# The last retention head's norm behind the combinations of the normalized input, and weight preparation behind copies of partial sums

## The chip, the cores and the metric

The kernel runs on one core of one Trainium2 chip. The metric is the device time of one execution in microseconds (us). TensorE is called PE in the profile, VectorE DVE, ScalarE ACT, GpSimd POOL and SyncE, which issues the transfers, SP.

## The reference, cut to what matters

One inference step of one decoder layer, for a prompt of 512 tokens and 8 single new tokens with states of their own. The kernel treats them as one matrix of N = 520 columns with 1024 channels.

```python
h = rms_norm(r, norm_mix_g)
rq, rk, rv, rg, gq, gf, gi, gg, a_ret, a_hg = split(h @ w_in)
o_r, s_ret = retention_chunked(rotary(rq), rotary(rk), rv, ...)       # 4 heads of 128 x 256
u_r = (o_r * rsqrt(mean(o_r * o_r) + EPS) * ret_norm_g * silu(rg)) @ w_up_ret
o_g, s_hg = gla_chunked(silu(gq), 1 - f, gi, log f, ...)              # 8 heads of 128 x 128
u_g = (o_g * rsqrt(mean(o_g * o_g) + EPS) * hg_norm_g * silu(gg)) @ w_up_hg
m = sigmoid(a_ret) * u_r + sigmoid(a_hg) * u_g
r = r + m @ w_o
r = r + square(relu(rms_norm(r, norm_mlp_g) @ w_ff1)) @ w_ff2
r = r + sigmoid(rms_norm(r, norm_ple_g) @ w_ple_gate) * (p_l @ w_ple_proj)
y = rms_norm(r, norm_final_g)
```

All of it is in float32. The change concerns the norm of the fourth retention head (in u_r), and the products for the two gates a_ret and a_hg.

## The kernel before

**Layout.** Activations lie with channels on the 128 partitions and the 520 columns along the free axis. A matrix product is made of units: one unit takes a 1024 x 128 block of a weight matrix, in 8 slots of 128 rows each. Weights and activations are each cut into a rounded half (H, wh) and the rest (L, wl); a product is wh*H + wh*L + wl*H, and the 520 columns go in two halves, so a slot is 6 matmuls and a unit 48 (`mm`, L232).

**Preparation.** A unit's weights arrive by a transfer into one of three `raw` buffers, and are then cut by `prep`: ScalarE copies them rounded into `wh` (L210) and VectorE subtracts (L215, `wl`). There are three `wh` and three `wl` buffers, and preparation runs two entries ahead of the product. After the cut the next transfer is issued.

**Pairs.** Some products (the gates a_ret and a_hg, and three quarters of ff1) are done two 128-column blocks at once with fewer multiplications (a Strassen-Winograd scheme). `sums` (L855 to L858) makes four combinations of the activations; `h_sums(kp)` does so for the normalized input, in five calls kp = 0 to 4: one adds H and L back together into `hn` (L942), forms the combinations into `hs`, and a call later cuts them into the two halves `hc` (rounded on ScalarE at L938, the rest on VectorE at L944). The tiles of `hc` lie in the places S8 and S9, S11 and S15, S13 and S14, S10 and S12. A pair runs in four steps, `run_pair(n, 0)` to `run_pair(n, 3)`, of 24, 24, 24 and 12 matmuls (`product`, L866); partial results X, Y and Z lie in PSUM. In step 0 ScalarE copies X (L881) and Z (L883) out, in step 1 it copies X again (L886) and VectorE adds Y to the first copy (L889), in step 2 VectorE subtracts X (L892), then the older copy of X from Z (L896). The next product that accumulates into X must wait until X has been read. The weights of each step are combinations too: `prep_pair` adds on VectorE (L172, into scratch space in `cst`), cuts on ScalarE (L166) and subtracts on VectorE (L168). `P.part` and `P.done` finish a result: for a gate a tanh (L967), and for a_hg a product on VectorE (L972); for ff1 relu (L1132), square (L1136) and a split (L587, L588).

**Order.** The order of the work is written out by hand: each engine runs its instructions in the order of the program text. `flow` lists units and steps of pairs. `at[u]` lists functions that run in the middle of unit u, after four of its slots, in the order in which they were appended. `run_unit` first prepares weights, then runs half the product, then the functions of `at[u]`, then the other half, and last the copy of the result out of PSUM. A set `prep_last` names steps of pairs that prepare weights in their middle and not at their start; before the change it holds step 2 of all eight gate pairs, and step 2 of the one ff1 pair that is followed by no ff2 unit in that step.

**Around the change.** Retention's heads 0 to 3 run in two groups P of two heads e. A head's last steps are `rt_out` (squares into `sq`, the gated result into `t`, both temporaries in the places S12 and S10), `rt_ext` (the 8 decode columns, then the split of the squares), `rt_norm` (a sum over partitions by four matmuls with ones, L579 and L580, then Ln, L569, and Exp, L571) and `rt_scale` (`t` times the result, L808, and its split, L587 and L588, into `orH` and `orL`). For head 3 these fall into the units of the first up-projection, `u_hg` to `u_hg + 4`, in whose middles the `h_sums` stand as well: `rt_norm` and `rt_scale` of head 3 and `h_sums(3)` stand in this order in `u_hg + 4`, `h_sums(4)` in `u_hg + 5`. Directly after that unit comes step 0 of the first gate pair. The up-projection's units copy their result into `xT` (L915), whose old content has been saved to DRAM (`xpark`). ScalarE holds one table of functions at a time; where an instruction needs another, a table load is put ahead of it, and `S.preload_act_table_set` puts one where it is called.

Of the kernel before, what the change touches and what calls it, by code (L numbers as in the profile page):

```python
# [19 lines left out]
N = T + NB  # L20
# [25 lines left out]
def decoder_step_kernel(  # L46
# [27 lines left out]
    V, S, G, PE = nc.vector, nc.scalar, nc.gpsimd, nc.tensor  # L74
# [13 lines left out]
    cst = cp.tile([128, C_END], F32, name="cst")  # L88
# [16 lines left out]
    def full(tag, dt=F32, name=None):  # L105
        return big.tile([128, 8, N], dt, tag=tag, name=name or tag)

    def pair(tag, name, dt=F32):
        return big.tile([128, 2, N], dt, tag=tag, name=name)

    def bank():
        return pss.tile([128, 512], F32, tag="s", name="s")
# [5 lines left out]
    at = defaultdict(list)  # L118
    extra = set()
    prep_last = set()  # L120
# [67 lines left out]
    def prep(engines=None, apart=False):  # L188


        if done["prep"] >= len(seq):
            return
        engines = engines or [(S, V)]
        u = seq[done["prep"]]
        done["prep"] += 1
        if not isinstance(u, int):
            prep_pair(*u)
            return
        r = raw_of.pop(u)
        if u in w_tags:  # L200
            wh, wl = (big.tile([128, 8, 128], F32R, tag=t, name="w6") for t in w_tags[u])
        else:
            wh = wp.tile([128, 8, 128], F32R, tag="wh", name="wh")
            wl = wp.tile([128, 8, 128], F32R, tag="wl", name="wl")
        w_of[u] = (wh, wl)
        n = 8 // len(engines)
        for i, (e0, e1) in enumerate(engines):
            k = slice(n * i, n * (i + 1))
            if e0 is S:
                S.activation(wh[:, k], r[:, k], AF.Copy)  # L210
            else:
                e0.tensor_copy(wh[:, k], r[:, k])
            if apart:
                yield
            e1.tensor_sub(wl[:, k], r[:, k], wh[:, k])  # L215
            if i < len(engines) - 1:
                yield
        load()

    def prep_all():  # L220
        for _ in prep():
            pass
# [52 lines left out]
    xT = full("B0", name="xT")  # L275
# [310 lines left out]
    def split(H, L, x):  # L586
        S.activation(H, x, AF.Copy)  # L587
        V.tensor_sub(L, x, H)  # L588
# [47 lines left out]
    rt = {}  # L636
# [120 lines left out]
    def rt_out(P, e):  # L757
        def go():
            hd = 2 * P + e
            vn, Sst, Q, g = rt["vn"], rt["S"], rt["Q", P][:, e], rt["g"]  # L760
            A = rt["A"][:, 0, 0:512]
            dma(ret_prompt[0, 0, hd], Sst[:, 3, :])
            sq = pair("S12", "rsq")
            t = pair("S10", "rt")
            for z in range(2):
                j = 2 * hd + z
                b = bank()
                zs = slice(z * 128, (z + 1) * 128)
                for c in range(4):
                    cs = slice(c * 128, (c + 1) * 128)  # L770
                    PE.matmul(b[:, cs], lhsT=vn[:, c, zs], rhs=A[:, cs], start=True, stop=c == 0)  # L771
                    if c:
                        PE.matmul(b[:, cs], lhsT=Sst[:, c - 1, zs], rhs=Q[:, cs], start=False, stop=True)
                S.activation(sq[:, z, 0:T], b, AF.Square)
                V.scalar_tensor_tensor(t[:, z, 0:T], in0=b, scalar=retg[:, j:j + 1], in1=g[:, z, 0:T],
                                       op0=ALU.mult, op1=ALU.mult)
                V.tensor_scalar(t[:, z, T:N], g[:, z, T:N], retg[:, j:j + 1], None, op0=ALU.mult)
            rt["sq"], rt["t"] = sq, t
        return go
# [14 lines left out]
    def rt_norm(P, e):  # L794
        def go():
            hd = 2 * P + e
            sq, t = rt["sq"], rt["t"]
            bs = ones_bc(rt["sqH"][:, 0], rt["sqH"][:, 1])
            r = sq[:, 0]
            rsqrt(r, bs, 1.0 / 256)  # L800
            rt["ng"] = t, r
        return go

    def rt_scale(P, e):
        def go():
            hd = 2 * P + e
            t, r = rt["ng"]
            V.tensor_tensor(t, t, r.unsqueeze(1).to_broadcast([128, 2, N]), op=ALU.mult)  # L808
            orH[hd] = pair(OSLOT[hd], "orH", F32R)
            orL[hd] = pair(f"S{4 + hd}", "orL", F32R) if hd else og["b"][:, 4:6]  # L810
            split(orH[hd], orL[hd], t)
        return go

    for P in range(2):
        b = len(units)
        for e in range(2):
            unit(W, RK + (2 * P + e) * 128, hk, hl, ev_rope(P, e, "K", KSCALE))
        for e in range(2):
            unit(W, RQ + (2 * P + e) * 128, hk, hl, ev_rope(P, e, "Q", 1.0))
        for e in range(2):  # L820
            for base, ev in ((RV, ev_rv), (RG, ev_rg)):
                for z in range(2):
                    unit(W, base + (2 * P + e) * 256 + z * 128, hk, hl, ev(P, e, z))
        for e in range(2):
            o = b + 4 * e
            at[o + 5].append(rt_scores(P, e))
            at[o + 6].append(rt_kT(P, e))
            at[o + 6].append(rt_vT(P, e))
            at[o + 7].append(rt_state(P, e))
            at[o + 8].append(rt_dec_add(P, e, 0))  # L830
            at[o + 9].append(rt_dec_add(P, e, 1))
            at[o + 10].append(rt_dec_out(P, e))
            at[o + 11].append(rt_ext(P, e))
            at[o + 12].append(rt_norm(P, e))
            at[o + 12].append(rt_scale(P, e))
        for e in range(2):
            at[b + 4 * e + 8].append(rt_out(P, e))

# [30 lines left out]
    def run_pair(n, i):  # L869

        P = pairs[n]
        if (n, i) not in prep_last:
            prep_all()
        if i == 0:
            P.t = P.begin()
            P.X, P.Z = bank()[:, 0:NH], bank()[:, 0:NH]
        X, Z = P.X, P.Z
        t1, t2 = P.t[:, 0], P.t[:, 1]
        if i == 0:
            product(n, 0, 0, "A11", X, True)  # L880
            S.activation(r1, X, AF.Copy)  # L881
            product(n, 0, 1, "S1", Z, True)
            S.activation(t2[:, z1], Z, AF.Copy)  # L883
        elif i == 1:
            product(n, 1, 0, "S2", X, False)
            S.activation(t2[:, z0], X, AF.Copy)  # L886
            Y = bank()[:, 0:NH]
            product(n, 1, 1, "A12", Y, True)
            V.tensor_tensor(t1[:, z0], r1, Y, op=ALU.add)  # L889
        elif i == 2:  # L890
            product(n, 2, 0, "S3", X, False)
            V.tensor_tensor(t2[:, z1], t2[:, z1], X, op=ALU.subtract)  # L892
            if (n, i) in prep_last:
                prep_all()
            product(n, 2, 1, "S4", Z, False)
            V.tensor_tensor(t2[:, z0], Z, t2[:, z0], op=ALU.subtract)  # L896
            P.part(1, slice(0, N), t2)
            P.done(1)
        else:
            P.part(0, z0, t1[:, z0])  # L900
            product(n, 3, 0, "A22", X, False)
            P.part(0, z1, X)
            P.done(0)
# [29 lines left out]
    def h_sums(kp):  # L933

        def go():
            if kp > 0:
                H, L = hc[kp - 1] = tuple(big.tile([128, 4, NH], F32R, tag=t, name="hc") for t in HTAGS[kp - 1])
                S.activation(H, hc["t"], AF.Copy)  # L938
            if kp < 4:
                n = pair("X2", "hn")  # L940
                for h in range(2):
                    V.tensor_tensor(n[:, h], hH[:, kp + 4 * h], hL[:, kp + 4 * h], op=ALU.add)  # L942
            if kp > 0:
                V.tensor_sub(L, hc["t"], H)  # L944
            if kp < 4:
                hc["t"] = big.tile([128, 4, NH], F32, tag="X0", name="hs")
                sums(hc["t"], n)
        return go
# [31 lines left out]
    u_hg = len(units)  # L980
# [4 lines left out]
        unit(w_up_ret[0], j * 128, lambda k: orH[k // 2][:, k % 2], lambda k: orL[k // 2][:, k % 2], ev_ur(j))  # L985
    for kp in range(5):
        at[u_hg + 1 + kp].append(h_sums(kp))
    flow += range(u_hg, u_hg + 6)
    gates = [gate_pair(j, c, c == A_RET) for j in range(4) for c in (A_RET, A_HG)]
    for n, u in zip(gates, [u_hg + 6, u_hg + 7, *range(u_ret, u_ret + 6)]):  # L990
        flow += [(n, 0), u, (n, 1), (n, 2), (n, 3)]
        prep_last.add((n, 2))
    flow += [u_ret + 6, u_ret + 7]


# [396 lines left out]
    for c in range(4):  # L1392
        t = big.tile([128, D], F32, tag=f"S{12 + c}", name=f"xn{c}")
# [79 lines left out]
    hd = pair("S1", "hd")[:, 0, 0:64].rearrange("p (k t) -> p k t", k=8)  # L1473
# [165 lines left out]
```

## Time and profile before

| | |
|---|---|
| median of 3 runs | 1101.16 us (1100.19 to 1101.61) |
| profiled execution, its own time | 1101.45 us |
| span of its profile, first to last instruction | 1099.6 us |
| mean granted clock of TensorE | 0.996 of full speed |
| busy: PE, DVE, ACT | 1081.8, 712.9, 509.7 us |
| the stage of the change: last up-projection units and gate pairs | about 440 to 612 us |

The profile is one execution. Its engines run side by side, so that busy times do not add up to the span: the engine that is busy nearly all the time sets it, and an idle time of another engine matters only where that engine ends up waiting for it. A row of a timeline gives the start of an instruction from the span's start, its length, the engine, the line of the kernel, the operation, the tile written and the tiles read; in brackets stands how long the engine had been idle before, and what ended that.

### The profile page before, as it was taken

The page shows a single profiled execution, that of the slowest core. Times are in us where ns is not written, and L with a number is a line of the kernel's source. Part 1 is how long each engine was busy: PE and PEld are TensorE (multiplying, and loading weights), DVE is VectorE, ACT ScalarE, POOL GpSimd, SP SyncE. Part 2 cuts the span into 40 slices and gives each one's busy share as a digit, 9 for nine tenths or more (in the row PEclk, how much of TensorE's full clock was granted, in tenths as well). Part 3 has the DMA queues.
Part 4 walks back from the last instruction along what each step waited for, and adds up shares of the span by engine and source line. Part 5 has one row for each costly group of instructions (what it writes and reads, how often), then busy time and mean ns, then how long its engine had stood idle before and what let it go on. Part 6 is the DMA issues. An engine that isn't in the chain of part 4 may idle for free.

```text
span 1099.6 us, 23412 instructions
## 1 busy us (share of the span) xinstructions
PE 1081.8 (98%) x10193; PEld 1061.1 (96%) x10193; DVE 712.9 (65%) x1113; ACT 509.7 (46%) x853; POOL 23.9 (2%) x19
## 2 busy tenths in 40 slices
PE   8999999999999999989999999999999999999997
PEld 8999999999999999989999999999999999999997
DVE  6566776858664854866677656776656665654565
ACT  6323534334254333555444335445555445544555
POOL 1000000000011011000000000000000000000001
PEclk9999999999999999999999999999999999999999
DMA  7556252443356456412343432232332332344302
GB/s 222 154 175 174 83 162 75 136 121 109 113 157 171 120 154 179 120 58 90 104 134 109 142 93 81 77 97 77 116 96 83 112 113 78 96 135 116 97 20 79
DMA packets 211847, 127.30 MB, mean 116 GB/s; under 512 B 4104, under 2 KB 209168, under 8 KB 211488
## 3 DMA queue, kind: packets, MB, share of 16 engines
q1 hardware_dynamic: 211744, 125.80, 38.8%
q8 instruction: 80, 1.31, 0.5%
q14 instruction: 23, 0.19, 0.1%
HBM read 112.02 MB, written 13.76 MB: 114 GB/s over the span
## 4 chain that ended last, share of the span: by engine, by line
PE 91%; DVE 5%; ACT 2%; issue 1%; DMA 0%; DVEq 0%; SPq 0%; ACTq 0%
PE m L232 57%; PE s L866 17%; PE m L1364 2%; PE s L1364 2%; PE s L369 1%; DVE wl L215 1%; PE s L488 1%; DVE comb L1070 1%; ACT wh L210 1%; PE s L549 1%; PE s L525 1%; PE s L771 1%; PE s L728 1%; PE s L232 1%; PE s L551 0%
## 5 line engine op out<-in xcount | busy, mean ns | idle before, releaser
L215 DVE TENSOR_TENSOR wl<-raw,wh 128x1024 fp32r<-128x1024 f32 (+1 forms) x125 | 155.4, 1245 | 80.2 <-ACT wh L210 79.4
L232 PE MATMUL m<-hH,wh 128*128 128x260 f32 x864 | 179.1, 289 | 0.0
L232 PE MATMUL m<-hH,wl 128*128 128x260 f32 x864 | 174.4, 283 | 0.0
L232 PE MATMUL m<-hL,wh 128*128 128x260 f32 x864 | 173.8, 283 | 0.0
L210 ACT ACTIVATE wh<-raw 128x1024 fp32r<-128x1024 f32 (+1 forms) x125 | 130.5, 1046 | 56.0 <-PE m L232 52.0
L232 PEld LDWEIGHTS m<-hH,wh 128*128 128x128 f32 x864 | 132.9, 189 | 2.5 <-issue 0.8
L232 PEld LDWEIGHTS m<-hH,wl 128*128 128x128 f32 x864 | 133.1, 188 | 0.0
L232 PEld LDWEIGHTS m<-hL,wh 128*128 128x128 f32 x864 | 133.1, 188 | 0.0
L866 PE MATMUL s<-comb,wh 128*128 128x260 f32 x672 | 122.4, 283 | 0.5 <-DVE comb L1070 0.5
L866 PEld LDWEIGHTS s<-comb,wh 128*128 128x128 f32 x672 | 103.9, 188 | 0.7 <-DVE comb L1070 0.7
L866 PE MATMUL s<-comb,wl 128*128 128x260 f32 x336 | 95.1, 283 | 0.0
L166 ACT ACTIVATE wh<-cst 128x512 fp32r<-128x512 f32 x80 | 50.5, 631 | 74.1 <-DVE cst L172 60.8
L232 PE MATMUL m<-fa,wh 128*128 128x260 f32 x384 | 67.0, 283 | 0.5 <-ACT fa L587 0.5
L232 PE MATMUL m<-oga,wh 128*128 128x260 f32 x384 | 65.5, 286 | 0.0
L168 DVE TENSOR_TENSOR wl<-cst,wh 128x512 fp32r<-128x512 f32 x80 | 55.2, 690 | 13.3 <-ACT wh L166 10.3
L866 PEld LDWEIGHTS s<-comb,wl 128*128 128x128 f32 x336 | 63.2, 188 | 0.0
L232 PEld LDWEIGHTS m<-oga,wh 128*128 128x128 f32 x384 | 54.7, 192 | 0.8 <-issue 0.8
L232 PEld LDWEIGHTS m<-fa,wh 128*128 128x128 f32 x384 | 54.7, 188 | 0.7 <-ACT fa L587 0.7
L866 PE MATMUL s<-hc,wh 128*128 128x260 f32 x256 | 48.8, 287 | 4.8 <-ACT hc L938 2.3
L232 PE MATMUL m<-fh,wl 128*128 128x260 f32 x256 | 51.3, 282 | 0.5 <-DVE wl L215 0.5
L232 PE MATMUL m<-fh,wh 128*128 128x260 f32 x256 | 51.6, 283 | 0.0
L232 PE MATMUL m<-fa,wl 128*128 128x260 f32 x256 | 51.5, 283 | 0.0
(375 smaller groups left out, 2322.8 us busy)
## 6 DMA issues: line engine op xcount, KB each, us to landing
raw<-in_w_in_dram SPq DMA_DIRECT2D x56, 512.0 KB, 4.3
raw<-in_w_ff_dram SPq DMA_DIRECT2D x40, 512.0 KB, 4.0
rawp<-in_w_ff_dram SPq DMA_DIRECT2D x24, 512.0 KB, 3.6
vbc<-vdd SPq DMA_DIRECT2D x16, 512.0 KB, 4.2
rawp<-in_w_in_dram SPq DMA_DIRECT2D x16, 512.0 KB, 4.6
Sd<-in_state_hgrn_dram SPq DMA_DIRECT2D x8, 512.0 KB, 5.5
out_dram<-Sd SPq DMA_DIRECT2D x8, 512.0 KB, 5.2
rSd<-in_state_ret_dram SPq DMA_DIRECT2D x8, 512.0 KB, 6.6
```

The lines of the kernel that those rows point to most:

```text
L166: S.activation(wh[:, 4 * h:4 * h + 4], x, AF.Copy)
L168: V.tensor_sub(wl[:, 4 * h:4 * h + 4], x, wh[:, 4 * h:4 * h + 4])
L210: S.activation(wh[:, k], r[:, k], AF.Copy)
L215: e1.tensor_sub(wl[:, k], r[:, k], wh[:, k])
L232: PE.matmul(ps[z], lhsT=a[:, k, :], rhs=b[:, z * NH:(z + 1) * NH], start=first and i == 0, stop=last and i == 2)
L369: PE.matmul(b[32 * j:32 * j + 32, 32 * hc:32 * hc + 32], lhsT=kx[:, h, o:o + 32], rhs=qx[:, h, o:o + 32], start=True, stop=True)
L488: PE.matmul(b[32 * i:32 * i + 32, :], lhsT=q[g], rhs=Sd[g][:, 4 * z:4 * z + 4, :], start=True, stop=True)
L525: PE.matmul(b[:, c * 128:(c + 1) * 128], lhsT=kn[:, h, c, :], rhs=vn[:, h, c, :], start=True, stop=True)
L549: PE.matmul(o, lhsT=vn[:, h, c, :], rhs=A[:, h * 4 + c, :], start=True, stop=c == 0)
L728: PE.matmul(b[:, c * 256:(c + 1) * 256], lhsT=kn[:, 2 * i + c, :], rhs=vn[:, 2 * i + c, :], start=True, stop=True)
L866: PE.matmul(out, lhsT=w[:, 4 * half + k, :], rhs=x, start=start and k == 0 and m == 0, stop=k == 3 and m == 2, skip_group_check=not start)
L1364: PE.matmul(ps, lhsT=w[:, k, :], rhs=x, start=k == 0 and n == 0, stop=k == 7 and n == 2)
```

## The change

It does four things. For head 3 the temporaries `sq` and `t` go from S12 and S10 into a stretch of `cst` whose constants have been used up and into rows 6 and 7 of `xT`. `rt_norm` and `rt_scale` of head 3 are appended after the `h_sums`: the norm behind `h_sums(3)` in `u_hg + 4`, the scaling behind `h_sums(4)` in `u_hg + 5`. Two table loads are written out, one in `u_hg + 1` with Ln and Exp, one after the scaling with the set that the gates' tanh uses. And in gate pairs step 1 also prepares weights in its middle, behind the copy L886; for every step 2 in `prep_last`, which includes the one ff1 pair, `P.part(1, ...)` and `P.done(1)` move from the end of step 2 into step 3, behind the preparation there.

```diff
@@ rt_out
-            sq = pair("S12", "rsq")
-            t = pair("S10", "rt")
+            if hd == 3:
+                sq = cst[:, 512:512 + 2 * N].rearrange("p (a n) -> p a n", a=2)
+                t = xT[:, 6:8]
+            else:
+                sq, t = pair("S12", "rsq"), pair("S10", "rt")
@@ the retention units
-            at[o + 12].append(rt_norm(P, e))
-            at[o + 12].append(rt_scale(P, e))
+            if P == 0 or e == 0:
+                at[o + 12].append(rt_norm(P, e))
+                at[o + 12].append(rt_scale(P, e))
@@ run_pair
             product(n, 1, 0, "S2", X, False)
             S.activation(t2[:, z0], X, AF.Copy)
+            if (n, i) in prep_last:
+                prep_all()
             Y = bank()[:, 0:NH]
...
             V.tensor_tensor(t2[:, z0], Z, t2[:, z0], op=ALU.subtract)
-            P.part(1, slice(0, N), t2)
-            P.done(1)
+            if (n, i) not in prep_last:
+                P.part(1, slice(0, N), t2)
+                P.done(1)
         else:
+            if (n, 2) in prep_last:
+                P.part(1, slice(0, N), t2)
+                P.done(1)
             P.part(0, z0, t1[:, z0])
@@ the up-projection and the gates
     for kp in range(5):
         at[u_hg + 1 + kp].append(h_sums(kp))
+    at[u_hg + 1].append(lambda: S.preload_act_table_set("natural_log_exp_and_others"))
+    at[u_hg + 4].append(rt_norm(1, 1))
+    at[u_hg + 5].append(rt_scale(1, 1))
+    at[u_hg + 5].append(lambda: S.preload_act_table_set("exp_and_others"))
...
-        prep_last.add((n, 2))
+        prep_last |= {(n, 1), (n, 2)}
```

## The prediction

> **What bounds the kernel now.** I read the page first, then the waits of TensorE, then the timelines of the places that these waits name. The first column of a timeline is the start in us from the span's start, the second the time from the first start to the last end of the row; the bracket is the idle time before it and what ended it.
>
> ```profile
> span 1099.6 us, 23412 instructions
> PE 1081.8 (98%) x10193; PEld 1061.1 (96%) x10193; DVE 712.9 (65%) x1113; ACT 509.7 (46%) x853; POOL 23.9 (2%) x19
> ```
>
> TensorE (PE) is busy for 1081.8 of 1099.6 us. The change takes no matmul away, so it can win only from TensorE's waits, or from time in which its matmuls run slowly. Its waits, over the whole span and then (last line) its weight loads from 476 to 620 us:
>
> ```profile
> PE s L866 <- ACT hc L938: 2.3, 1, 2.3
> PE s L866 <- DVE hc L944: 1.9, 2, 1.0
> ...
> PE m L232 <- DVE wl L215: 0.5, 1, 0.5
> ```
>
> ```profile
> PEld s L866 <- ACT gt L886: 1.9, 6, 0.3
> ```
>
> Three places appear: one long stop on the combinations `hc` (L938 is the rounded half, L944 the rest), six equal stops on the copy in L886, and one on a weight preparation (L215). The change touches the queues ahead of all three. The waits understate what each costs, so I size each by its period on TensorE. These are starts of matmuls of the gate pairs:
>
> ```profile
> 476.79 0.28 PE L866 MATMUL s<-hH,wh 128*128 128x260 f32 x1
> ...
> 482.98 0.39 PE L866 MATMUL s<-hc,wh 128*128 128x260 f32 x1 [2.26 <-ACT hc L938]
> ...
> 491.84 0.40 PE L866 MATMUL s<-hc,wh 128*128 128x260 f32 x2
> ...
> 499.03 0.28 PE L866 MATMUL s<-hH,wh 128*128 128x260 f32 x1
> ...
> 507.69 0.40 PE L866 MATMUL s<-hc,wh 128*128 128x260 f32 x2
> ```
>
> From 476.79 to 491.84 TensorE runs step 0 of the first pair and one unit, 24 + 48 = 72 matmuls, in 15.05 us. From 499.03 to 507.69 it runs the same 72 of the second pair in 8.66 us, 0.120 each. **The first stop costs 15.05 - 8.66 = 6.39 us.**
>
> Why it stops is on VectorE (DVE) and ScalarE (ACT), here in order of time on each:
>
> ```profile
> 470.05 0.69 DVE L168 TENSOR_TENSOR wl<-cst,wh 128x512 fp32r<-128x512 f32 x1
> 474.16 1.24 DVE L808 TENSOR_TENSOR rt<-rt,rsq 128x1040 f32<-128x1040 f32 x1 [3.42 <-ACT rsq L571]
> 476.54 1.24 DVE L588 TENSOR_TENSOR orL<-rt,orH 128x1040 fp32r<-128x1040 f32 x1 [1.14 <-ACT orH L587]
> 477.70 1.31 DVE L942 TENSOR_TENSOR hn<-hH,hL 128x520 f32<-128x520 f32 x2
> ...
> 481.34 0.43 DVE L858 TENSOR_TENSOR hs<-hs,hn 128x260 f32<-128x260 f32 x1
> 481.68 1.22 DVE L215 TENSOR_TENSOR wl<-raw,wh 128x1024 fp32r<-128x1024 f32 x1
> 482.96 1.24 DVE L944 TENSOR_TENSOR hc<-hs,hc 128x1040 fp32r<-128x1040 f32 x1
> ```
>
> ```profile
> 470.04 1.28 ACT L569 ACT_TABLE_LOAD   x1
> ...
> 472.19 1.28 ACT L571 ACT_TABLE_LOAD   x1
> 473.49 0.64 ACT L571 ACTIVATE rsq<-rsq 128x520 f32<-128x520 f32 x1
> ...
> 476.41 1.06 ACT L938 ACTIVATE hc<-hs 128x1040 fp32r<-128x1040 f32 x1
> 477.38 0.58 ACT L915 ACTIVATE xT<-m 128x520 f32<-128x520 f32 x1
> ...
> 481.86 1.07 ACT L938 ACTIVATE hc<-hs 128x1040 fp32r<-128x1040 f32 x1 [2.95 <-DVE hs L858]
> ```
>
> Retention's last norm (Ln, Exp, the product in L808, the split in L588) sits ahead of the fourth `hn` sum. VectorE idles 3.42 us for the Exp, behind two table loads, and 1.14 us for ScalarE's half of the split. The last combination is done at 482.96 + 1.24 = 484.20, while TensorE wants it soon after 479.
>
> **Part 1, the norm behind the combinations.** Nothing ahead of 470.05 moves. The temporaries of head 3 now lie in `cst` and `xT`, so the last `hc` tiles in S10 and S12 do not wait for the norm; all earlier readers of those places are over. From there I lay the same instructions out again with the same durations. VectorE: the block L942 to L858 takes 481.34 + 0.43 - 477.70 = 4.07 us and starts at 470.7, so it ends at 474.8. ScalarE: the third rounded `hc` (1.06) runs at 470.0 to 471.0, then Ln (472.19 - 470.04 - 1.28 = 0.87), Exp (0.64) and the copy L915 (0.58) to 473.1, then the weight cast L210 (1.04 in a row below) to 474.1. Then, with both engines past them, the fourth rounded `hc` (1.07) from 474.8 to 475.9, L215 beside it, and L944 to 477.2. TensorE asks for the rounded half as matmul 21 after 476.79 (counted from zero), at 479.3, and for the rest at 479.4. The combination is there 2.2 us early: the stop goes whole.
>
> What is late next? rt_scale now comes last: L808 to 478.4, ScalarE's split to 479.5, L588 to 480.7, and the table load added after it (1.28) to 480.8. Behind this wait the copy L915 and the preparation of the pair's second step: two casts like L166 (0.61, in a row below) and two subtractions like L168 (0.69), with two additions of about the same length ahead. These end near 483.5; TensorE reaches that step at 476.79 + 8.66 = 485.45. So 2 us of cover remain; each microsecond beyond it would be a microsecond of wait. The norm's own result is used only by units after the second pair. The four matmuls of the norm keep their place in TensorE's order.
>
> The other added table load stands in the second unit of the stage. Its price is that of the rows above, 1.28 us, and the copy behind it in ScalarE's queue has idle time ahead of it:
>
> ```profile
> 451.86 0.61 ACT L915 ACTIVATE xT<-m 128x520 f32<-128x520 f32 x1 [4.20 <-PE m L232]
> ```
>
> So it costs nothing; without that cover it would be 1.28 us on ScalarE. That Ln and Exp then need no load of their own is seen where the kernel already preloads:
>
> ```profile
> 672.81 1.28 ACT L1175 ACT_TABLE_LOAD   x1
> 674.10 0.84 ACT L569 ACTIVATE x<-s,eps 128x260 f32<-128x260 f32 x2
> 674.98 0.64 ACT L571 ACTIVATE x<-x 128x520 f32<-128x520 f32 x1
> ```
>
> If Exp reloaded all the same, the chain would slip by 1.28 us and stay within the 2.2.
>
> The 6.39 us hold more than waiting. Right after the stop the matmuls are slow (columns: window, its length, busy time of each engine, granted clock, DMA):
>
> ```profile
> 484.86:487.46 2.60, 2.60 (x14) 2.60 (x13) 2.51 (x5) 2.60 (x6) 0.00 (x0) 0.50 0.77 217
> ```
>
> At clock 0.50 those 2.60 us cost about 1.3, which belongs to the stop if the stop caused it. The waits there are 2.3 and twice up to 1.0 us, so I take it as caused, and count all 6.39. The other bound is 6.39 - 1.3 = 5.1. The Trainium skill, "TensorE: Matmul & The Clock Gate", Part 1, says that the clock falls to half after at least one idle window of about 3.4 us. No single wait here is that long, so by that rule read strictly the slow stretch would stay and the sum would be 1.3 us smaller; the trace's clock fell all the same, just behind the three waits.
>
> **Part 2, the copy L886 ahead of the preparation, in all eight gate pairs.** The third pair's queue, and the starts of the same step in two successive pairs:
>
> ```profile
> 525.17 0.64 ACT L926 ACTIVATE oga<-thr 128x520 fp32r<-128x520 f32 x1 [3.25 <-DVE thr L924]
> 525.71 0.61 ACT L166 ACTIVATE wh<-cst 128x512 fp32r<-128x512 f32 x1
> 526.23 0.37 ACT L886 ACTIVATE gt<-s 128x260 f32<-128x260 f32 x1
> ```
>
> ```profile
> 523.50 0.40 PE L866 MATMUL s<-hc,wh 128*128 128x260 f32 x2
> ...
> 539.69 0.40 PE L866 MATMUL s<-hc,wh 128*128 128x260 f32 x2
> ```
>
> The product that reads X next may start at 523.50 + 24 x 0.120 = 526.4, but L886 ends at 526.60. With the cast L166 behind it, L886 starts at 525.7 and ends at 526.1: 0.3 us early. The period with the wait is 539.69 - 523.50 = 16.19, the one without it 507.69 - 491.84 = 15.85: 0.34 us in each of six pairs, **2.04 us**. The cast then ends at about 526.6 instead of 526.3, and its subtraction follows; they are wanted only in the last step, which starts 24 matmuls (2.9 us) after 526.4.
>
> The other part of the edit moves the tanh of the finished half, and what follows it, behind the next unit's preparation. In the gate pairs nothing on TensorE waits for it: zero on this path.
>
> **Part 3, the same edit in one ff1 pair.** The pair ahead of the second ff2 quarter is in `prep_last` too, so its relu, square and split move behind the next unit's preparation (L210, L215):
>
> ```profile
> 805.61 0.64 ACT L1132 ACTIVATE hid<-hid 128x520 f32<-128x520 f32 x1 [1.10 <-DVE hid L896]
> ...
> 806.95 0.64 ACT L587 ACTIVATE fh<-hid 128x520 fp32r<-128x520 f32 x1
> 807.49 1.04 ACT L210 ACTIVATE wh<-raw 128x1024 fp32r<-128x1024 f32 x1
> ```
>
> ```profile
> 805.50 0.41 PE L866 MATMUL s<-comb,wh 128*128 128x260 f32 x2
> ...
> 815.20 0.40 PE L866 MATMUL s<-comb,wh 128*128 128x260 f32 x2
> ```
>
> L210 could start at about 804.5, inside the idle time that the first row shows (1.10 us up to 805.61), and L215 would end near 806.9. TensorE wants the weights at 805.50 + 24 x 0.120 = 808.4. These 72 matmuls take 9.70 us against 8.66: **1.04 us**. The displaced split of `fh` is read as the unit's seventh slot, over 4 us into it, so it hides.
>
> **Sum.** 6.39 + 2.04 + 1.04 = 9.47 us. The profiled execution took 1101.45 us, 1.85 more than its span; less 9.47 that is 1091.98. The median of the three runs shown, 1101.16, is 0.29 below the profiled one, so I forecast **1091.7**.
>
> **Rivals.**
> - *Parts 2 and 3 fail.* For it: ScalarE's margin in part 2 is only 0.3 us and the copy still stands behind L926. Against: the cast that goes is 0.5 us of queue. Lost alone, part 2 leaves 1093.7, part 3 1092.7, both 1094.8. Chance 0.13.
> - *The slow stretch is not the stop's.* The half clock stays: 1093.0. Chance 0.04.
> - *The combinations stay late*, so that the change doesn't do what it says: a dependence that the trace does not show (on all of `cst` or `xT`, say) holds L942 or L944 back. Beyond 2.2 us each microsecond is paid; a slip of 5.2 leaves a 3 us stop and 1094.7, and the whole stop back gives 1098.1. Chance 0.06.
> - *Slower: the preparation for the last step comes late.* The cast now waits for a product to end, and the additions into `gt` queue behind its subtraction; the last step's product waits for L892, the subtraction that reads X.
>
> ```profile
> 528.41 0.42 DVE L892 TENSOR_TENSOR gt<-gt,s 128x260 f32<-128x260 f32 x1 [0.93 <-PE s L866]
> ```
>
> L892 ends at 528.83, TensorE wants X about 24 x 0.120 = 2.9 us after the end of L886 at 526.60, at 529.5; so there are 0.7 us, plus the 0.93 that VectorE idles before it. Only a slip over 1.6 us costs anything. To be over 0.2% (2.2 us, about what a measurement of this kernel can tell from no change) slower, eight pairs must lose 9.47 + 2.2 us, 1.5 each: a slip of 3.1 us where I count 0.2. It would give 1103.4 or more. Chance 0.03.
> - *Within 0.2%*: the saved time is lost again at a later wait, 1099 to 1103. The earlier weight loads speak against it. Chance 0.03.
>
> The forecast itself has 0.71, from 1090.4 to 1093.0 with the run-to-run spread of 1.4 us. The range takes in part 2 or part 3 failing and the slow clock: 1090.3 to 1094.0. Faster by over 0.2% 0.94, within 0.03, slower 0.03.
>
> **What would show it.** Right: no wait of TensorE on L938 or L944, clock 1.0 through the first pair, its 72 matmuls in 8.7 us; L942 to L858 of the fourth sum ahead of L808; no table load at L569 or L571 for the last head; pair periods all 15.85; L210 ahead of L1132 near 804 less the shift, and no wait on L215. Wrong: a wait on L886, on L892 or on `wh` in the last steps, or the same total with a new stop behind the first pair.

## The result and the profile after

The changed kernel takes 1091.02 us (median of 4 runs, 1090.35 to 1091.65), the kernel before 1101.22 us (median of 4, 1100.19 to 1101.61). The ratio is 0.9909, with a 95% interval of 0.9892 to 0.9926: about 0.9% faster, clear of noise. The profiled execution took 1090.35 us.

The page of the changed kernel, its first lines:

```profile
span 1088.6 us, 23418 instructions
PE 1075.7 (99%) x10193; PEld 1057.0 (97%) x10193; DVE 711.2 (65%) x1113; ACT 509.8 (47%) x853; POOL 23.9 (2%) x19
```

The same number of matmuls in a span that is 11.0 us shorter. The longest waits of TensorE, over the whole span:

```profile
PE m L1470 <- DMA xs<-in_x_sample_dram: 3.4, 1, 3.4
PE m L1291 <- DVE sqs L1263: 0.9, 1, 0.9
PE s L870 <- DVE comb L1084: 0.5, 1, 0.5
```

No wait on `hc` is left, none on the weights of an ff2 unit (L215), none on the copy of X. What remains is the wait on the load at the start and waits outside the gate pairs.

**Not all of the 11.0 us are the change's.** The start of the program scatters. The chain of waits, in order of time (start, length, what), has these pieces in the kernel before and in the changed kernel; the first is the first run of 24 matmuls, the last a stretch of ff2 units near the end:

```profile
28.19 2.86 PE m L232 x24
...
1003.75 34.41 PE m L232 x288
```

```profile
26.80 2.86 PE m L232 x24
...
992.68 34.41 PE m L232 x288
```

The profile of before began its first units 1.39 us later, in a part of the program that the change does not touch. In the thirteen profiles of this study the first piece starts either at 26.8 to 27.1 or at 28.0 to 28.4 us, whatever the kernel. So I compare kernels by the rest of the span behind this piece as well: 1099.6 - 28.19 = 1071.41 before, 1088.6 - 26.80 = 1061.80 after. **The change is worth 9.6 us**; the medians differ by 10.2, and the scatter at the start is large enough for the difference between the two.

**Where they came from.** VectorE of the changed kernel around the end of the up-projection units, then ScalarE (L952 and L954 are the old L942 and L944, L811 the old L808, L862 the old L858, L948 the old L938):

```profile
469.32 1.30 DVE L952 TENSOR_TENSOR hn<-hH,hL 128x520 f32<-128x520 f32 x2
...
472.95 0.43 DVE L862 TENSOR_TENSOR hs<-hs,hn 128x260 f32<-128x260 f32 x1
473.30 1.22 DVE L215 TENSOR_TENSOR wl<-raw,wh 128x1024 fp32r<-128x1024 f32 x1
474.53 1.24 DVE L954 TENSOR_TENSOR hc<-hs,hc 128x1040 fp32r<-128x1040 f32 x1
475.69 1.23 DVE L811 TENSOR_TENSOR xT<-xT,cst 128x1040 f32<-128x1040 f32 x1
478.06 1.24 DVE L588 TENSOR_TENSOR orL<-xT,orH 128x1040 fp32r<-128x1040 f32 x1 [1.14 <-ACT orH L587]
...
481.28 0.69 DVE L168 TENSOR_TENSOR wl<-rawp,wh 128x512 fp32r<-128x512 f32 x1
```

```profile
470.40 0.64 ACT L571 ACTIVATE cst<-cst 128x520 f32<-128x520 f32 x1
...
473.42 1.08 ACT L948 ACTIVATE hc<-hs 128x1040 fp32r<-128x1040 f32 x1 [0.93 <-DVE hs L862]
476.95 1.07 ACT L587 ACTIVATE orH<-xT 128x1040 fp32r<-128x1040 f32 x1 [2.46 <-DVE xT L811]
478.05 1.28 ACT L1001 ACT_TABLE_LOAD   x1
```

The sums follow the earlier work without a gap, the last combination is done at 474.53 + 1.24 = 475.77, and the scaling comes behind it. The 1.14 us for ScalarE's half of the split are still there, but what waits behind them has cover: the preparation of the pair's second step ends at 481.28 + 0.69 = 481.97 (last row of VectorE), 2.1 us before TensorE reaches that step at 484.09. TensorE of the changed kernel, first matmul of the first gate pair, first on `hc`, and first of its step 1:

```profile
475.44 0.28 PE L870 MATMUL s<-hH,wh 128*128 128x260 f32 x1
...
476.88 0.41 PE L870 MATMUL s<-hc,wh 128*128 128x260 f32 x2
...
484.09 0.40 PE L870 MATMUL s<-hc,wh 128*128 128x260 f32 x2
```

The 72 matmuls take 484.09 - 475.44 = 8.65 us, where they took 15.05. In the gate pairs, step 1 of one pair to step 1 of the next is now 15.81 us (chain of waits):

```profile
515.92 10.09 PE s L870 x84
526.00 5.73 PE m L232 x48
531.73 10.08 PE s L870 x84
```

A whole pair, 84 matmuls, is one piece without a break. Before, each of the six later pairs was cut behind 23 matmuls by the copy L886, as here in the third pair:

```profile
523.66 2.66 PE s L866 x23
526.33 0.28 ACT gt L886
```

ScalarE at the ff1 pair that changed:

```profile
793.88 0.63 ACT L166 ACTIVATE wh<-cst 128x512 fp32r<-128x512 f32 x1 [1.96 <-DVE cst L172]
794.42 1.04 ACT L210 ACTIVATE wh<-raw 128x1024 fp32r<-128x1024 f32 x1
795.61 0.64 ACT L1146 ACTIVATE hid<-hid 128x520 f32<-128x520 f32 x1
```

The weight cast L210 fills the gap that stood ahead of the relu.

### The profile page after: what moved, and what is told of

Its sections match the earlier page's. It is cut to its first block, busy times and chain, and to the rows that moved or that the text cites. A ratio compares the mean times of both kernels' runs of the same rounds, so it can differ in the third digit from the quotient of the medians.

```text
span 1088.6 us, 23418 instructions
## 1 busy us (share of the span) xinstructions
PE 1075.7 (99%) x10193; PEld 1057.0 (97%) x10193; DVE 711.2 (65%) x1113; ACT 509.8 (47%) x853; POOL 23.9 (2%) x19
## 4 chain that ended last, share of the span: by engine, by line
PE 96%; DVE 2%; ACT 1%; DMA 0%; issue 0%; SPq 0%; DVEq 0%
PE m L232 62%; PE s L870 18%; PE m L1378 2%; PE s L1378 2%; PE s L369 1%; PE s L488 1%; PE s L774 1%; PE s L549 1%; PE s L525 1%; PE s L728 1%; PE s L232 1%; PE s L551 0%; PE s L776 0%; PE s L352 0%; PE s L512 0%; PE s L464 0%
## 5 line engine op out<-in xcount | busy, mean ns | idle before, releaser
L215 DVE TENSOR_TENSOR wl<-raw,wh 128x1024 fp32r<-128x1024 f32 (+1 forms) x125 | 154.5, 1238 | 72.9 <-ACT wh L210 72.2
L210 ACT ACTIVATE wh<-raw 128x1024 fp32r<-128x1024 f32 (+1 forms) x125 | 130.5, 1045 | 57.6 <-PE m L232 51.8
L168 DVE TENSOR_TENSOR wl<-cst,wh 128x512 fp32r<-128x512 f32 x80 | 55.2, 690 | 15.3 <-ACT wh L166 11.7
L232 PE MATMUL m<-fl,wh 128*128 128x260 f32 x256 | 51.5, 282 | 0.0
```

What stands on the lines that cost most here:

```text
L168: V.tensor_sub(wl[:, 4 * h:4 * h + 4], x, wh[:, 4 * h:4 * h + 4])
L232: PE.matmul(ps[z], lhsT=a[:, k, :], rhs=b[:, z * NH:(z + 1) * NH], start=first and i == 0, stop=last and i == 2)
```

## The experiments

Each ratio is to runs of the kernel before on the same chip, whose medians were 1101.30 to 1101.57 us for the experiments. "Rest" is the span less the start of the first run of 24 matmuls, from the one profile of each kernel; the four kernels that show none of the three stops (changed, no table loads written, deferral in one pair, both preparations in step 2) agree in it within 0.06 us. "Stretch" is the time from the first matmul on `hc` to the first of step 1, which takes 7.21 us in the changed kernel.

| kernel | median us | ratio to before, 95% | rest us | rest against the changed kernel | stretch us |
|---|---|---|---|---|---|
| before | 1101.22 | | 1071.41 | +9.61 | 13.61 |
| changed | 1091.02 | 0.9909 (0.9892 to 0.9926) | 1061.80 | | 7.21 |
| norm only | 1093.97 | 0.9933 (0.9920 to 0.9945) | 1065.09 | +3.29 | |
| queue only | 1098.22 | 0.9966 (0.9953 to 0.9978) | 1068.16 | +6.36 | |
| no table loads written | 1090.45 | 0.9902 (0.9886 to 0.9917) | 1061.74 | -0.06 | |
| table loads only | 1097.19 | 0.9956 (0.9944 to 0.9969) | 1067.32 | +5.52 | 9.44 |
| no deferral | 1092.69 | 0.9917 (0.9904 to 0.9931) | 1062.83 | +1.03 | |
| deferral in one pair | 1091.05 | 0.9905 (0.9891 to 0.9918) | 1061.75 | -0.05 | |
| four extra writes | 1092.72 | 0.9920 (0.9906 to 0.9934) | 1063.93 | +2.13 | 9.47 |
| five extra writes | 1095.47 | 0.9948 (0.9932 to 0.9964) | 1066.59 | +4.79 | 12.09 |
| six extra writes | 1097.62 | 0.9964 (0.9951 to 0.9976) | 1067.68 | +5.88 | 13.18 |
| scaling first | 1092.92 | 0.9919 (0.9905 to 0.9933) | 1063.03 | +1.23 | 8.48 |
| both preparations in step 2 | 1090.56 | 0.9903 (0.9889 to 0.9917) | 1061.78 | -0.02 | |

**The two halves alone.** First the norm, its temporaries and table loads, without the edit of `run_pair`. The changed kernel with that edit taken back:

```diff
             S.activation(t2[:, z0], X, AF.Copy)
-            if (n, i) in prep_last:
-                prep_all()
...
-            if (n, i) not in prep_last:
-                P.part(1, slice(0, N), t2)
-                P.done(1)
+            P.part(1, slice(0, N), t2)
+            P.done(1)
         else:
-            if (n, 2) in prep_last:
-                P.part(1, slice(0, N), t2)
-                P.done(1)
...
-        prep_last |= {(n, 1), (n, 2)}
+        prep_last.add((n, 2))
```

> Only the norm, its temporaries and the table loads are moved; the gate pairs and the ff1 pair queue as before. My theory (three separate costs that add up): the stop on hc goes whole, the 72 matmuls from the first pair's step 0 take 8.65 us instead of 15.05, and the six waits of 0.3 us on the copy of X and the one on the ff1 weights stay: 1101.2 - 6.4 = 1094.8 us. Rival (the queue turn in the pairs is needed for the gain of the first): the stop comes back in part in the first pair, 1096 or more.

Its rest is 1071.41 - 1065.09 = 6.32 us below that of before. The median fell by 7.6 against its own runs of before, a difference that is again of the size of the scatter at the start. The stop on `hc` is gone whole and the others stay, as this row of TensorE's waits shows:

```profile
PE m L232 <- DVE wl L215: 0.5, 1, 0.5
```

Then the edit of `run_pair` alone, on the kernel before:

```diff
             S.activation(t2[:, z0], X, AF.Copy)
+            if (n, i) in prep_last:
+                prep_all()
...
-            P.part(1, slice(0, N), t2)
-            P.done(1)
+            if (n, i) not in prep_last:
+                P.part(1, slice(0, N), t2)
+                P.done(1)
         else:
+            if (n, 2) in prep_last:
+                P.part(1, slice(0, N), t2)
+                P.done(1)
...
-        prep_last.add((n, 2))
+        prep_last |= {(n, 1), (n, 2)}
```

> Only the queue of the pairs is changed (preparation behind the copy of X in step 1, tanh or relu of the first half behind the preparation of step 3); the norm stays ahead of the combinations. Theory: the stop on hc stays at 15.05 us for 72 matmuls, six periods fall from 16.19 to 15.81 and the ff1 stretch from 9.70 to 8.65: 2.3 + 1.05 = 3.3 us, 1097.9 us. Rival (the first stop hides part of these): under 2 us, 1099 or more.

Its rest is 3.25 us below that of before. The waits on `hc` are unchanged in it (L944 and L950 are the old L938 and L944), and the others are gone:

```profile
PE s L866 <- ACT hc L944: 2.3, 1, 2.3
PE s L866 <- DVE hc L950: 1.9, 2, 1.0
```

6.32 + 3.25 = 9.57, against 9.61 for both together: the two halves add up, and neither needs the other. The move of the temporaries is in every kernel with the new order; what it does alone was not run.

**The table loads.** The changed kernel without the two written loads, so that Ln and Exp each load again:

```diff
-    at[u_hg + 1].append(lambda: S.preload_act_table_set("natural_log_exp_and_others"))
...
-    at[u_hg + 5].append(lambda: S.preload_act_table_set("exp_and_others"))
```

> The changed kernel without the two written table loads, so that Ln and Exp load their tables again inside the norm. Theory (the order is what gains, the loads only use cover): ScalarE's chain slips by two loads of 1.28 us, the last combination is ready at about 477.8 where TensorE asks at 478.1 on the time axis of the changed kernel's profile: no stop, 1091.0 us as the changed kernel, at most 0.5 more. Rival (the loads are part of the gain): a stop of 1 to 2.6 us, 1092 to 1094.

There is no loss: the rest is 0.06 us shorter. The last combination and the place where TensorE asks for it, in this kernel:

```profile
476.52 1.24 DVE L954 TENSOR_TENSOR hc<-hs,hc 128x1040 fp32r<-128x1040 f32 x1
```

```profile
478.12 0.40 PE L870 MATMUL s<-hc,wh 128*128 128x260 f32 x2
```

It ends at 477.76, about 2 us later than with the written loads, and still ahead of the second matmul of that row. The other way round, the kernel before with the written loads and nothing else:

```diff
         at[u_hg + 1 + kp].append(h_sums(kp))
+    at[u_hg + 1].append(lambda: S.preload_act_table_set("natural_log_exp_and_others"))
+    at[u_hg + 5].append(lambda: S.preload_act_table_set("exp_and_others"))
```

> The kernel before with the two written table loads alone; norm ahead of the combinations as before. Theory: the chain from Ln to the last combination loses two loads of 1.28 us, so the stop shrinks from 5.2 us of waiting to 2.6; the half clock behind it stays if 2.6 us of stop still cause it (1101.2 - 2.6 = 1098.6) and goes if not (1097.4). Rival (the loads hide behind other waits): no gain, 1101.2.

Its rest is 4.09 us below that of before, a little more than the larger of the two expected gains (1101.2 - 1097.4 = 3.8). TensorE in it:

```profile
479.00 0.39 PE L866 MATMUL s<-hc,wh 128*128 128x260 f32 x1 [0.81 <-ACT hc L938]
480.28 0.39 PE L866 MATMUL s<-hc,wh 128*128 128x260 f32 x1 [0.89 <-DVE hc L944]
```

and behind this stop (window, its length, busy time of each engine, granted clock, DMA):

```profile
480.60:483.00 2.40, 2.40 (x22) 2.40 (x21) 2.30 (x5) 2.40 (x7) 0.00 (x0) 1.00 0.67 188
```

The chain is two loads shorter, a stop of about 2.2 us stays (9.44 - 7.21), and the clock holds in this execution. It may not do so each time: four of the five runs show a mean clock of 0.998, but the slowest, at 1097.90 us, shows 0.995, and no trace of it was kept. So the loads alone are worth 4.1 of the 6.4 us, and nothing once the order is changed: they work on the same stop.

**The deferral.** The changed kernel with `P.part(1)` and `P.done(1)` left at the end of step 2, and then with the deferral in the ff1 pair alone:

```diff
-            if (n, i) not in prep_last:
-                P.part(1, slice(0, N), t2)
-                P.done(1)
+            P.part(1, slice(0, N), t2)
+            P.done(1)
...
-            if (n, 2) in prep_last:
-                P.part(1, slice(0, N), t2)
-                P.done(1)
```

> The changed kernel, but with P.part(1) and P.done(1) left at the end of step 2 in all pairs. Theory (the deferral gains only in the one ff1 pair): the pair periods stay 15.81 us, the ff1 stretch of 72 matmuls goes back from 8.65 to 9.7 us: 1091.0 + 1.05 = 1092.1 us. Rival (the deferral is what ends the waits on the copy of X as well): 2.3 us more, 1094.3.

```diff
-            if (n, i) not in prep_last:
+            if (n, i) not in prep_last or n < 8:
...
-            if (n, 2) in prep_last:
+            if (n, 2) in prep_last and n >= 8:
```

> The changed kernel with the deferral in the one ff1 pair only, none in the eight gate pairs. Theory: nothing on TensorE waits for the deferred tanh in the gate pairs, so periods of 15.81 us and 1091.0 us as the changed kernel. Rival (the earlier preparation in the gate pairs is worth something): periods above 15.81, more than 0.3 us in total.

Without any deferral the rest is 1.03 us longer, and with it in the one ff1 pair alone it is that of the changed kernel. The gate pairs of the latter run in the same period (548.79 - 532.98 = 15.81):

```profile
532.98 10.09 PE s L870 x84
...
548.79 10.09 PE s L870 x84
```

Moving the tanh in eight gate pairs is worth nothing; moving one relu is worth a microsecond, because that preparation was the one that TensorE waited for.

**The margin, and the clock behind a stop.** The changed kernel, with ScalarE's half of the last combination written five, six or seven times instead of once:

```diff
-                S.activation(H, hc["t"], AF.Copy)
+                for _ in range(4 + 1 if kp == 4 else 1):      # in the others 5 + 1, 6 + 1
+                    S.activation(H, hc["t"], AF.Copy)
```

> The changed kernel with ScalarE's rounded half of the fourth combination written five times instead of once, so that it is ready 4 x 0.97 = 3.9 us later. Theory: the measured margin (rounded half ready 3.5 us early, the rest 2.3 us early) is eaten and a stop of about 1.6 us appears, at two waits; too short to lower the clock: 1092.6 us. Rival (any stop on the clock's edge costs the half clock too): 1.2 us more, 1093.8.

> As the kernel with four extra copies, with six: 5.8 us later. Theory (the half clock is caused by the stop, as before the change): a stop of about 3.5 us, and behind it 2 to 3 us at clock 0.50 that cost 1.2 us: 1091.0 + 3.5 + 1.2 = 1095.7 us. Rival (the slow stretch is not the stop's, or needs one wait of over 3.4 us): clock 1.0 behind the stop, 1094.5 us.

> The changed kernel with five extra writes of the rounded half of the last combination, between the kernels with four (stop 2.3 us, clock 1.0 behind it) and with six (stop 4.5 us, clock 0.54). Each extra write adds 1.1 us: a stop of 3.4 us. Theory (the clock looks at how much of a stretch of about 3.4 us is idle, wherever the waits are cut): half clock behind it in some executions and not in others, 1094.4 or 1095.8 us. Rival (the longest single wait counts): clock 1.0, 1094.4 us in all.

In the first two a size was off: an extra write costs 1.1 us and not 0.97, as this row of the kernel with four shows (five writes in 5.50 us):

```profile
473.56 5.50 ACT L949 ACTIVATE hc<-hs 128x1040 fp32r<-128x1040 f32 x5 [0.93 <-DVE hs L862]
```

So four give a stop of 9.47 - 7.21 = 2.26 us, where 1.6 was expected, and the kernel with six took 1097.62 us, where 1095.7 was expected; part of this is the start, which was a late one in its profile (28.12 us). TensorE's waits at the stop, and the clock behind it, with four extra writes:

```profile
479.11 0.39 PE L870 MATMUL s<-hc,wh 128*128 128x260 f32 x1 [0.85 <-ACT hc L949]
480.39 0.39 PE L870 MATMUL s<-hc,wh 128*128 128x260 f32 x1 [0.89 <-DVE hc L955]
```

```profile
480.60:483.00 2.40, 2.40 (x21) 2.40 (x21) 1.26 (x2) 1.46 (x2) 0.00 (x0) 1.00 0.03 7
```

with five:

```profile
480.32 0.39 PE L870 MATMUL s<-hc,wh 128*128 128x260 f32 x1 [1.94 <-ACT hc L949]
481.60 0.39 PE L870 MATMUL s<-hc,wh 128*128 128x260 f32 x1 [0.89 <-DVE hc L955]
```

```profile
482.00:486.00 4.00, 4.00 (x23) 4.00 (x23) 2.86 (x4) 3.24 (x4) 0.00 (x0) 0.59 0.01 4
```

and with six:

```profile
484.00:488.00 4.00, 4.00 (x22) 4.00 (x22) 2.86 (x4) 3.08 (x4) 0.00 (x0) 0.57 0.02 4
```

From four to five writes the stretch grows by 12.09 - 9.47 = 2.62 us for 1.1 us of delay, from five to six by 1.09. So 1.5 us of the step are the clock, which fell to about a half: the slow stretch behind a stop is caused by the stop. It fell with waits of 1.94 and 0.89 us, so it does not need a single wait of 3.4 us.

What it does need stays open. With four writes it held behind 0.85 + 0.89 = 1.74 us of waits, and in the kernel below, with the scaling first, behind a single wait of 1.00 us. So both the longest wait and the sum of the waits still fit. It is not shown either that the clock falls in every execution of the kernel with five writes, since one was profiled. That one, with the early start and the fallen clock, took 1095.49 us; a held clock and a late start would give about 1095.49 - 1.5 + 1.2 = 1095.2, too close to the runs at 1095.38 and 1095.44 to tell them apart.

**Half of the new order.** The changed kernel with the scaling ahead of the last combination:

```diff
-    at[u_hg + 5].append(rt_scale(1, 1))
+    at[u_hg + 5].insert(0, rt_scale(1, 1))
```

> The changed kernel, but with the scaling of head 3 ahead of the last combination in the last up-projection unit that carries one (the norm stays behind the third). Theory (each instruction ahead of the last combination is paid once the 2.3 us of margin are used): the product and the split with its round trip over ScalarE put 3.6 us ahead, so the last combination's rest comes at about 479.3 where TensorE asks at 478.1 on the changed kernel's axis: a stop of 1.2 us, no slow clock behind it, 1092.2 us. Rival (only the norm's place matters): 1091.0 us.

The stretch is 8.48 us, 1.27 more, and the rest 1.23 more. TensorE waits once:

```profile
480.61 0.39 PE L870 MATMUL s<-hc,wh 128*128 128x260 f32 x1 [1.00 <-DVE hc L954]
```

and behind this wait the clock holds:

```profile
482.00:485.00 3.00, 3.00 (x27) 3.00 (x26) 3.00 (x5) 2.00 (x5) 0.00 (x0) 1.00 0.58 172
```

So the place of the scaling matters too: ahead of the last combination it costs 1.2 of the 6.4 us. The norm itself, behind the third combination and ahead of the last in both kernels, was not moved further.

**The slower rival, driven further.** The preparation for a pair's last step moved from step 1 into step 2:

```diff
             S.activation(t2[:, z0], X, AF.Copy)
-            if (n, i) in prep_last:
-                prep_all()
...
             V.tensor_tensor(t2[:, z1], t2[:, z1], X, op=ALU.subtract)
+            if (n, 1) in prep_last:
+                prep_all()
             if (n, i) in prep_last:
                 prep_all()
```

> The changed kernel with the preparation for the last step of a pair moved still later, from the middle of step 1 into the middle of step 2, behind the subtraction of X and ahead of the preparation that stands there. It tests the rival on the slower side of the prediction. Theory (the queue has slack): the rest of the weights is ready 0.1 to 0.3 us before TensorE asks for it, so periods stay 15.81 us, at most 0.2 more in each of eight pairs: 1091.0 to 1092.6 us. Rival (late weights): waits on the weights at the start of each last step of 0.5 us or more, 1095 us or more.

The rest is that of the changed kernel, and the period is still 15.81 (532.05 - 516.24 in its chain of waits). VectorE's part of that preparation there:

```profile
520.61 0.43 DVE L896 TENSOR_TENSOR gt<-gt,s 128x260 f32<-128x260 f32 x1 [1.02 <-PE s L870]
520.95 0.69 DVE L168 TENSOR_TENSOR wl<-cst,wh 128x512 fp32r<-128x512 f32 x1
```

and the first matmul of the last step on TensorE:

```profile
521.84 0.28 PE L870 MATMUL s<-hH,wh 128*128 128x260 f32 x1
```

The subtraction that cuts the weights (L168) ends at 520.95 + 0.69 = 521.64, ahead of the step that reads its result. So late weights are no danger even one step later. The prediction's slack, though, was that of another instruction, the subtraction that reads X (the old L892), and this run takes the preparation out of its way. For that one the changed kernel itself is the evidence:

```profile
520.29 0.43 DVE L898 TENSOR_TENSOR gt<-gt,s 128x260 f32<-128x260 f32 x1 [0.38 <-PE s L870]
```

```profile
521.53 0.28 PE L870 MATMUL s<-hH,wh 128*128 128x260 f32 x1
```

That subtraction ends at 520.72, 0.8 us before the last step's product into X begins. With the 0.38 us that VectorE idles before it, 1.2 us of cover are left of the 1.6 that the prediction found: the change took 0.4, where 0.2 was counted.

## Why the prediction was right

**The first stop, 6.39 us: measured 6.40** (15.05 to 8.65), and 6.32 when that half runs alone. The layout of the new order by old durations held to a few tenths: the combination was expected 2.2 us ahead of TensorE's request and came 2.3 us ahead (done at 475.77; TensorE reads it ten matmuls after its first on `hc`, at 476.88 + 10 x 0.12 = 478.08). That the slow stretch belongs to the stop was a choice between two bounds, on the ground that it came right behind the waits; the extra writes now show it. The other bound, 5.1, would have been wrong. The Trainium skill, "TensorE: Matmul & The Clock Gate", Part 1, has the clock fall after at least one idle window of about 3.4 us. Read strictly, that does not agree with these traces: the clock fell with single waits of at most 2.26 us in the kernel before, and of at most 1.94 us with five writes.

**The six waits, 2.04 us: measured 2.28.** The step that was mis-sized is the period without the wait. I took 15.85 from the pair that runs beside an up-projection unit of the first matrix; the pairs that waited run beside units of the second, and theirs is 15.81. The saving is 16.19 - 15.81 = 0.38 in each of six.

**The ff1 pair, 1.04 us: measured 1.03**, by taking it out.

**The sum, 9.47: measured 9.6** in the rest of the span, and the forecast of 1091.7 lay 0.7 above the median. The sum accounts for 0.1 of that; the remainder is within the scatter of the start. Charging the two table loads and the deferral in the gate pairs at nothing was right in the order that the change makes.

**The rivals.** That parts 2 and 3 fail, that the combinations stay late, that the slow clock stays, and that the time is lost again later: each would show a wait or a period that the profile after does not have. The slower rival did not come: late weights cost nothing even a step later, and the subtraction that reads X kept about 1.2 us of its cover, less than was counted but enough.

## What to carry to other kernels

Where an engine that is busy 98% of the time stops, follow the stop back through the queues of the others. Look there for work that stands ahead of what the engine needs and is itself needed only later. Here such work waited for its own round trips (for Exp, then for the split between two engines) and held up everything behind it, while moving it cost nothing. Size such a stop by the period of the same work elsewhere in the trace, not by the listed waits: 4.2 us of waits were worth 6.4. About 1.5 us of the difference are the clock that fell behind them; and even with the clock held, 1.74 us of listed waits were a stop of 2.26. And several fixes of one stop do not add up: the table loads written early were worth 4.1 us alone, the order 6.4 without them, both together no more.

## What the runs showed of the hardware

The granted clock of TensorE held at 1.00 behind waits of 0.85 and 0.89 us close together and behind a single wait of 1.00 us. It fell to about a half behind waits of 1.94 and 0.89 us; its mean of 0.59 over 4.00 us is, at 0.50, an estimated 0.41 x 4.00 / 0.50 = 3.3 us. The step cost 1.5 us. Five writes of one tile by ScalarE took 5.50 us, 1.1 each. A single such write is listed at 1.08 in the changed kernel, and in the kernel before the copy behind one starts 0.97 after it (476.41 and 477.38). The start of this program lasts 26.8 to 27.1 us in some executions and 28.0 to 28.4 in others, for the same instructions, which is larger than the smallest effect measured here; why was not tried.
